# Output projection as seven half-size products for eight, with the norm's row factors moved to the gate products

## The chip, the cores and the metric

The kernel runs on one core of one Trainium2 chip. The metric is the device time of one launch in microseconds; the profiled execution's trace is counted from the start of its span. TensorE multiplies matrices, VectorE (DVE), ScalarE (ACT) and GpSimd (POOL) work on tiles of 128 partitions, and SyncE (SP) and GpSimd issue transfers.

## The reference

One layer of a decoder trunk, with 1024 rows, a width of 1024 and all data in float32. What bears on the change is the end of the mixing sub-layer and the start of the feed-forward:

```python
gates = jax.nn.sigmoid(bg + b_gate[l])
merged = None
for i, y_b in enumerate((y_gla, y_fox, y_mem)):
    term = gates[..., i * D_MODEL:(i + 1) * D_MODEL] * (y_b @ w_branch[l, i])
    merged = term if merged is None else merged + term
x = x + merged @ w_out[l]
h2 = _rmsnorm(x, g_ffn[l])                      # x * rsqrt(mean(x*x) + EPS) * g
x = x + (jax.nn.silu(h2 @ w_ffn_gate[l]) * (h2 @ w_ffn_up[l])) @ w_ffn_down[l]
```

The feed-forward width is 2816. The row factor of the norm (one number for each of the 1024 rows) can be applied to `h2` or, since it is constant along the summed dimension, to the products.

## The kernel before

Activations lie transposed: 128 channels on the partitions, the 1024 rows along the free dimension, in two halves of 512 (`H2`). Every float32 product is three matmuls of 128x512 (`mm3`, lines 844, 846, 848): each operand is split into a rounded high half (a ScalarE cast, line 872) and a low half (a VectorE subtraction, line 873), and high x high, high x low and low x high are summed in one of eight PSUM banks.

The work follows in stages. The merge (`merge_lane`, from about 786 us) multiplies each of the three branches by its projection and by its gate; VectorE forms gate x product (L906), GpSimd adds it to the sum (L907), and for the last branch ScalarE and VectorE split the finished sum (L909, L910). The output projection (`out_half`, 927 to 1019 us) computes for each half of the rows and each of 8 strips of 128 output channels a sum over 8 input strips, adds it to the input tile `x`, stores it (L966) and sums its squares. `half_factors` turns the sums of squares of a half into row factors: narrow matmuls (L978), a power on GpSimd (L103), a diagonal matrix (L980) and one wide matmul (L984). The first half's factors are known during the second half of the projection, and the operands of the first half, B11 and B21, are scaled and split there. The second half's factors are formed after the projection.

The feed-forward works in pairs of 128-channel strips. `products` computes a pair by seven products of half size in place of eight (a Winograd form, its order in `SEQ`): the weights' combinations S1 to S4 are formed and split by `Strip` (its parts `a`, `b`, `c_sums`, `c`, `d` are called between the products of the strip before), and the activations' combinations T1 to T4 are formed once, before the first pair's products use them (`staggered`, `t2_sum` and the functions beside it). Each product sums over 4 input strips, 12 matmuls in all. `Pair.gate` and `Pair.up` read the banks: some products are copied out by ScalarE (L1107), others are added by VectorE; the gate gets Silu (L1126), the up product is multiplied by the gate. `Pair.store` writes seven combinations to memory for the down projection (from 1454 us), which is of the same form.

TensorE's order is written out by hand for the whole kernel; VectorE's from the first product of the feed-forward on, ScalarE's from the third strip on. Before that, VectorE and ScalarE take the order that the planner of the framework sets. Each engine works its queue in order, and a transfer waits in its issuing engine's queue until its tile is free.

## Time and profile before

| what | us |
|---|---|
| median of 3 runs | 1678.42 (1677.35 to 1678.88) |
| the profiled execution | 1678.62 |
| its span | 1676.9 |
| TensorE busy in the span | 1648.2 |
| VectorE busy | 971.4 |
| ScalarE busy | 631.4 |
| GpSimd busy | 185.7 |

The span is the time from the first to the last instruction of the trace; the profiled execution's own time is 1.7 us more. Busy time of TensorE counts overlapping matmuls once, and a matmul's end is modelled, so the distance between starts of matmuls says more than a matmul's duration.

### The profile page before, as it was taken

To read this page: it belongs to the slowest core of one execution; us is meant where nothing else is said; L and a number is where in the kernel's file an instruction comes from. 1 tells how busy PE (TensorE), PEld (TensorE's weight loads), DVE (VectorE), ACT (ScalarE), POOL (GpSimd) and SP (SyncE) were. 2 spreads that over 40 slices of the span, in tenths; PEclk is the share of its full clock that TensorE was granted. 3 is DMA by queue.
4 is the path that set the end of the run, shared out by engine and by line. 5 is a ranking of instruction groups with operands and counts; after the bars stand their busy time and mean duration, and the time that the engine had idled before them with its cause. 6 is when DMAs were issued, how large, how long until landed. Compare 5 with 4: busy or idle time off the path is not lost.

```text
span 1676.9 us, 21943 instructions
## 1 busy us (share of the span) xinstructions
PE 1648.2 (98%) x8411; PEld 1391.6 (83%) x8411; DVE 971.4 (58%) x1537; ACT 631.4 (38%) x1078; POOL 185.7 (11%) x225
## 2 busy tenths in 40 slices
PE   8999999999999999999999999999999999999999
PEld 6889987878879999998887787788888888787877
DVE  8544464154244655554447477866666666748673
ACT  7334454223223444443113344433333333544340
POOL 2000000000010100100044110111121121100000
PEclk9999999999999999999999999999999999999999
DMA  6431121112121221114556631455464455965761
GB/s 226 145 121 63 52 95 59 32 59 87 54 72 53 88 70 54 39 60 156 188 197 199 222 120 57 148 172 163 145 195 150 155 168 168 314 204 195 241 227 57
DMA packets 127321, 220.79 MB, mean 132 GB/s; under 512 B 11552, under 2 KB 71472, under 8 KB 127216
## 3 DMA queue, kind: packets, MB, share of 16 engines
q1 hardware_dynamic: 116256, 183.47, 33.4%
q0 software_dynamic: 10960, 35.92, 6.4%
q8 instruction: 66, 1.08, 0.3%
q14 instruction: 39, 0.32, 0.1%
HBM read 160.30 MB, written 59.05 MB: 131 GB/s over the span
## 4 chain that ended last, share of the span: by engine, by line
PE 85%; DVE 6%; DMA 5%; ACT 2%; issue 1%; SPq 0%; POOL 0%; DVEq 0%; ACTq 0%
PE ps L846 14%; PE ps L848 14%; PE ps L844 14%; PE pm L234 4%; PE pt L155 4%; PE pm L236 4%; PE pm L235 4%; PE pt L156 4%; PE pt L157 4%; PE pm L197 2%; PE pm L201 2%; PE pm L199 2%; PE at L791 1%; DMA hbl<-act_d 1%; DMA raw<-y_d 1%
## 5 line engine op out<-in xcount | busy, mean ns | idle before, releaser
L846 PE MATMUL ps<-hbl,h 128*128 128x512 f32 x520 | 204.1, 393 | 3.4 <-DVE hbl L932 1.8
L844 PE MATMUL ps<-hbh,h 128*128 128x512 f32 x520 | 203.0, 390 | 2.5 <-ACT h L872 1.4
L848 PE MATMUL ps<-hbh,l 128*128 128x512 f32 x520 | 203.7, 392 | 0.5 <-DVE l L873 0.5
L872 ACT CAST h<-w 128x1024 fp32r<-128x1024 f32 (+3 forms) x111 | 97.9, 895 | 175.0 <-DVE w L932 89.8
L234 PE MATMUL pm<-whi,hh 128*128 128x384 f32 (+2 forms) x512 | 162.2, 317 | 0.0
L236 PE MATMUL pm<-whi,hl 128*128 128x384 f32 (+2 forms) x512 | 158.8, 310 | 0.0
L235 PE MATMUL pm<-wlo,hh 128*128 128x384 f32 (+2 forms) x512 | 158.8, 310 | 0.0
L155 PE MATMUL pt<-hh,whi 128*128 128x512 f32 x352 | 142.3, 404 | 0.0
L157 PE MATMUL pt<-hh,wlo 128*128 128x512 f32 x352 | 138.1, 392 | 0.0
L156 PE MATMUL pt<-hl,whi 128*128 128x512 f32 x352 | 138.1, 392 | 0.0
L873 DVE TENSOR_TENSOR l<-w,h 128x1024 fp32r<-128x1024 f32 (+3 forms) x111 | 114.5, 1034 | 37.5 <-ACT h L872 37.4
L846 PEld LDWEIGHTS ps<-hbl,h 128*128 128x128 f32 x520 | 97.8, 188 | 27.1 <-DVE hbl L873 3.5
L844 PEld LDWEIGHTS ps<-hbh,h 128*128 128x128 f32 x520 | 97.8, 188 | 24.1 <-ACT h L872 1.8
L848 PEld LDWEIGHTS ps<-hbh,l 128*128 128x128 f32 x520 | 97.9, 188 | 21.5 <-DVE l L873 1.3
L234 PEld LDWEIGHTS pm<-whi,hh 128*128 128x128 f32 x512 | 96.3, 188 | 2.6
L235 PEld LDWEIGHTS pm<-wlo,hh 128*128 128x128 f32 x512 | 96.4, 188 | 2.5
L846 PE MATMUL ps<-hal,ah 128*128 128x512 f32 x248 | 97.4, 393 | 0.9 <-DVE hal L873 0.7
L848 PE MATMUL ps<-hah,al 128*128 128x512 f32 x248 | 97.2, 392 | 0.0
L844 PE MATMUL ps<-hah,ah 128*128 128x512 f32 x248 | 96.6, 389 | 0.0
L236 PEld LDWEIGHTS pm<-whi,hl 128*128 128x128 f32 x512 | 96.2, 188 | 0.0
L187 DVE TENSOR_TENSOR wlo<-raw,whi 128x512 fp32r<-128x512 f32 (+2 forms) x64 | 48.3, 756 | 78.6 <-ACT whi L186 78.0
L931 DVE TENSOR_TENSOR acc<-ps,acc 128x512 f32<-128x512 f32 x68 | 46.8, 688 | 66.9 <-PE ps L848 66.9
(358 smaller groups left out, 3528.8 us busy)
## 6 DMA issues: line engine op xcount, KB each, us to landing
w<-in_wfd SPq DMA_DIRECT2D x52, 256.0 KB, 3.9
tg<-tg_d SPq DMA_DIRECT2D x24, 512.0 KB, 3.6
w<-in_wfu SPq DMA_DIRECT2D x23, 512.0 KB, 4.7
w<-in_wfg SPq DMA_DIRECT2D x23, 512.0 KB, 4.1
raw<-in_wT SPq DMA_DIRECT2D x22, 512.0 KB, 4.3
tg_d<-gz SPq DMA_DIRECT2D x22, 512.0 KB, 2.9
act_d<-T POOLq DMA_DIRECT2D x44, 256.0 KB, 3.8
sum_d<-w POOLq DMA_DIRECT2D x44, 256.0 KB, 3.4
```

What stands on the lines that cost most here:

```text
L155: nc.tensor.matmul(ps, hi[:, ks], hh[k][:, sl], start=k == 0, stop=False)
L156: nc.tensor.matmul(ps, hi[:, ks], hl[k][:, sl], start=False, stop=False)
L157: nc.tensor.matmul(ps, lo[:, ks], hh[k][:, sl], start=False, stop=k == KT - 1)
L187: nc.vector.tensor_tensor(lo[:, :n], raw[:, :n], hi[:, :n].bitcast(F32), ALU.subtract)
L234: nc.tensor.matmul(ps[:, :n], hh[k][:, ms], hi, start=k == 0, stop=False)
L235: nc.tensor.matmul(ps[:, :n], hh[k][:, ms], lo, start=False, stop=False)
L236: nc.tensor.matmul(ps[:, :n], hl[k][:, ms], hi, start=False, stop=k == KT - 1)
L844: nc.tensor.matmul(ps, hi, a, start=first, stop=False, skip_group_check=more)
L846: nc.tensor.matmul(ps, hi, b, start=False, stop=False, skip_group_check=more)
L848: nc.tensor.matmul(ps, lo, a, start=False, stop=last, skip_group_check=more)
L872: nc.scalar.copy(hi, raw)
L873: nc.vector.tensor_tensor(lo, raw, hi.bitcast(F32), ALU.subtract)
```

## The change

The output projection takes the form of the feed-forward: strips j and j+4 of the output make a pair, and each pair is seven products over 4 input strips in place of eight. The merged sum is split for it into seven combinations: B11, T1, B21 and T2 in the merge's last branch, T3, B22 and T4 during the first strip of the projection (`half_split`). The weights of the projection are laid out by pair and go through `Strip`. The order of VectorE's and ScalarE's work is written out from the projection on. Low halves of weights, square sums and gains are put on a list (`kept`) and issued some products later (`weigh`).

The feed-forward's operands carry only the gain of the norm. Sums of squares for both halves are gathered in one tile `rb`, which becomes the row factors while the first products of the feed-forward run. Each gate product is multiplied by the factor before Silu (VectorE) and after it (GpSimd), the second for the up product's factor. Differences T1, T3 and T4 of the first operands are formed by GpSimd. Tiles `x` are loaded in the order of the pairs, the first strip's (0,1), (4,1) and (4,0) on GpSimd's queue and all others on SyncE's; staging slots for the activations are named by combination (four each) in place of three shared rings. The branch weights are laid out so that the merge takes its strips in the order j, j+4.

The diff, cut to its core (of the functions that it removes, the code is above):

```diff
     ap_ = pool(root, "acc", side="right")
+    fp_ = pool(root, "factors", side="right")
+    rb = fp_.tile([P, S], F32, name="rb")
+    nc.gpsimd.memset(rb, 0.0)
...
+    one = lambda pl, tag, dt=F32R, n=1, w=S: pl.tile([P, w], dt, tag=tag, bufs=n, name=tag)
+    a4 = lambda: (one(xp, "ah"), one(xp, "al"))
+    s2_ = lambda: (one(xp, "s2h"), one(xp, "s2l"))
+    hp1 = pool(root, "h2a")
+    hp2 = pool(root, "h2b")
+    RING = {"B11": hp1, "B21": hp1, "T2": hp2, "T1": hp2}
+    slot = lambda name: tuple(RING[name].tile([P, 512], F32R, tag=name + x, bufs=4, name=name + x) for x in "hl")
+    cell = lambda name: ap_.tile([P, 512], F32, tag="cell", bufs=16, name=name)
+    add = lambda o, a, b: nc.vector.tensor_tensor(o, a, b, ALU.add)
+    sub = lambda o, a, b: nc.vector.tensor_tensor(o, a, b, ALU.subtract)
+    mul = lambda o, a, b: nc.vector.tensor_tensor(o, a, b, ALU.mult)
+    cells = lambda name: {(j, h): cell(name) for js, h in ((range(4), 0), (range(4), 1), (range(4, 8), 1), (range(4, 8), 0))
+                          for j in js}
+    am = cells("am")
+    mg = {}
+    def half_split(name, k, raw, pool_lo=False, late=None):
+        mg[name, k] = hi, lo = slot(name)
+        if pool_lo:
+            nc.scalar.activation(raw, raw, AF.Copy, scale=0.5)
+            nc.scalar.copy(hi, raw)
+            nc.gpsimd.tensor_tensor(lo, raw, hi.bitcast(F32), ALU.subtract)
+            return
+        nc.scalar.activation(hi, raw, AF.Copy, scale=0.5)
+        make = lambda: nc.vector.scalar_tensor_tensor(lo, raw, 0.5, hi.bitcast(F32), ALU.mult, ALU.subtract)
+        make() if late is None else late.append(make)
     def merge_lane():
...
-                    j = jj * 2 + j2
+                    j = jj + 4 * j2
...
-                            nc.gpsimd.tensor_tensor(acc[j][h], acc[j][h], tg[:, s], ALU.add)
-                        if n == 2:
-                            nc.scalar.activation(mgh[j][:, s], acc[j][h], AF.Copy, scale=0.5)
-                            nc.vector.scalar_tensor_tensor(mgl[j][:, s], acc[j][h], 0.5, mgh[j][:, s].bitcast(F32),
-                                                           ALU.mult, ALU.subtract)
+                            nc.gpsimd.tensor_tensor(am[j, h], am[j, h], tg[:, s], ALU.add)
+                    if n == 2 and j2 == 0:
+                        m11, m12 = am[jj, 0], am[jj, 1]
+                        half_split("B11", jj, m11)
+                        sub(m11, m12, m11)
+                        half_split("T1", jj, m11)
+                    if n == 2 and j2 == 1:
+                        m21, m22 = am[jj + 4, 0], am[jj + 4, 1]
+                        half_split("B21", jj, m21)
+                        sub(m11, m22, m11)
+                        half_split("T2", jj, m11)
+                        sub(m12, m22, m12)
+                        nc.gpsimd.tensor_tensor(m21, m21, m11, ALU.subtract)
...
+    wo_a, wo_s = a4(), s2_()
+    ra = wp.tile([P, S], F32, tag="wr", bufs=2, name="raw")
+    rb_, sa = (one(wx, "wx", F32, 2) for i in range(2))
+    nc.sync.dma_start(ra, wout[0][:, 0:S])
+    nc.sync.dma_start(rb_, wout[0][:, S:2 * S])
+    split(*wo_a, ra)
+    add(sa[:, 512:], rb_[:, :512], rb_[:, 512:])
+    sub(sa[:, :512], sa[:, 512:], ra[:, :512])
+    split(*wo_s, sa)
...
+        def split(self, dst, raw, late):
+            if late is None:
+                return split(*dst, raw)
+            nc.scalar.copy(dst[0], raw)
+            late.append([1, lambda: sub(dst[1], raw, dst[0].bitcast(F32))])
+            return dst
+        def a(self, late=None):
             if not self.at:
+                h, l = self.split(a4(), self.ra, late)
                 self.at = {"A11": (h, l, 0), "A12": (h, l, 512)}
+        def b_sums(self, eng=nc.vector):
             sa, ra, rb_ = w4(), self.ra, self.rb
             self.s2, s1 = sa[:, :512], sa[:, 512:]
+            eng.tensor_tensor(s1, rb_[:, :512], rb_[:, 512:], ALU.add)
+            eng.tensor_tensor(self.s2, s1, ra[:, :512], ALU.subtract)
+            return sa
+        def b(self, sa=None, own=True, late=None):
+            sa = self.b_sums() if sa is None else sa
+            h, l = self.split(s2_() if own else a4(), sa, late)
             self.at.update({"S2": (h, l, 0), "S1": (h, l, 512)})
+        def c_sums(self, eng=nc.vector):
             self.sb = w4()
+            eng.tensor_tensor(self.sb[:, 512:], self.ra[:, 512:], self.s2, ALU.subtract)
+            eng.tensor_tensor(self.sb[:, :512], self.ra[:, :512], self.rb[:, :512], ALU.subtract)
+        def c(self, own=True, late=None):
+            h, l = self.split(s3_() if own else s2_(), self.sb, late)
             self.at.update({"S3": (h, l, 0), "S4": (h, l, 512)})
+        def d(self, late=None):
+            h, l = self.split(d2_(), self.rb[:, 512:], late)
             self.at["A22"] = (h, l, 0)
...
+            def then(i, l):
+                def act():
+                    t, r = g[i][l], rb[:, H2[l]]
+                    mul(t, t, r)
+                    nc.scalar.activation(t, t, AF.Silu)
+                    nc.gpsimd.tensor_tensor(t, t, r, ALU.mult)
+                if late is None:
+                    act()
+                else:
+                    late.append(act)
             def last(ps):
+                t, r = cell("t"), rb[:, H2[0]]
+                g[1][0] = t
+                mul(t, ps, r)
+                nc.scalar.activation(t, t, AF.Silu)
+                nc.gpsimd.tensor_tensor(t, t, r, ALU.mult)
+            return products(w, hB, 4, self.reads(g, then, last))
...
+    ve = tc.manual_schedule(engines={mybir.EngineType.DVE, mybir.EngineType.Activation})
+    ve.__enter__()
+    wo = [Strip(w) for w in wout]
+    wo[0].at = {"A11": (*wo_a, 0), "A12": (*wo_a, 512), "S2": (*wo_s, 0), "S1": (*wo_s, 512)}
+    g0, u0, g1 = Strip(wfg[0]), Strip(wfu[0]), Strip(wfg[1])
     pairs = [Pair(), Pair()]
-    g0.b()
-    g0.c_sums()
-    g0.c()
+    late = []
+    x1 = cells("x1")
+    kept = []
+    def load_x(j, h, eng=nc.sync):
+        eng.dma_start(x1[j, h], xT[j][:, H2[h]])
+    def ready(j, h):
+        x, sl = x1[j, h], H2[h]
+        nc.gpsimd.dma_start(x_d[j][h], x)
+        sq = bank8()
+        nc.scalar.activation(sq, x, AF.Square)
+        kept.append([1, lambda: add(rb[:, sl], rb[:, sl], sq)])
+        kept.append([0, lambda: nc.scalar.activation(x, x, AF.Copy, scale=gain(j))])
+    def weigh(age):
+        for y in list(kept):
+            y[0] += 1
+            if y[0] > age:
+                y[1]()
+                kept.remove(y)
+    def out_reads(j):
+        def plus(i, h, last):
+            def read(ps):
+                x = x1[j + 4 * i, h]
+                add(x, x, ps)
+                if last:
+                    ready(j + 4 * i, h)
+            return read
+        return [plus(0, 0, False), plus(0, 0, True), plus(0, 1, False), plus(1, 1, False), plus(1, 1, True),
+                plus(0, 1, True), plus(1, 0, True)]
+    def op(name, k, raw):
+        hops[name, k] = split(*slot(name), raw)
+    def ops_of(name, ks, make=None):
+        where = {"B11": (0, 0), "T1": (0, 0), "T2": (0, 0), "T3": (0, 1), "B21": (4, 0), "T4": (4, 0), "B22": (4, 1)}
+        j, h = where[name]
+        lo = None
+        for k in ks:
+            raw = x1[k + j, h]
+            if make:
+                make(k)
+            hi, l = hops[name, k] = slot(name)
+            nc.scalar.copy(hi, raw)
+            if lo:
+                lo()
+            lo = lambda l=l, raw=raw, hi=hi: sub(l, raw, hi.bitcast(F32))
+        lo()
+    t1 = lambda k: nc.gpsimd.tensor_tensor(x1[k, 0], x1[k, 1], x1[k, 0], ALU.subtract)
+    t2 = lambda k: sub(x1[k, 0], x1[k + 4, 1], x1[k, 0])
+    t3 = lambda k: nc.gpsimd.tensor_tensor(x1[k, 1], x1[k + 4, 1], x1[k, 1], ALU.subtract)
+    t4 = lambda k: nc.gpsimd.tensor_tensor(x1[k + 4, 0], x1[k + 4, 0], x1[k, 0], ALU.subtract)
+    first = range(3)
+    wo[0].load()
+    load_x(0, 0)
+    wo[1].load()
+    mB = lambda name, k: mg[name, k]
+    e1 = None
+    for n in range(4):
+        q = products(wo[n].get, mB, 4, out_reads(n))
+        nxt = wo[n + 1] if n < 3 else g0
+        for i, (_, _, name) in enumerate(SEQ):
+            go(q, 4)
+            weigh(2)
+            if n == 0 and i == 0:
+                los = []
+                for k in range(4):
+                    half_split("T3", k, am[k, 1], late=los)
+                wo[0].b_sums()
+                wo[0].c_sums()
+                wo[0].c(late=kept)
+                for lo in los:
+                    lo()
+                load_x(0, 1, nc.gpsimd)
+                for k in range(4):
+                    half_split("B22", k, am[k + 4, 1], True)
+                weigh(1)
+            if n == 0 and i == 1:
+                wo[0].d(kept)
+            if n == 0 and i == 2:
+                load_x(4, 1, nc.gpsimd)
+            if n == 0 and i == 3:
+                for k in range(4):
+                    half_split("T4", k, am[k + 4, 0])
+                load_x(4, 0, nc.gpsimd)
+            if n == 3:
+                if i == 1:
+                    ops_of("B11", first)
+                    for k in first:
+                        t1(k)
+                if i == 3:
+                    ops_of("B21", first)
+                    e1 = w4(F32R), w4(F32R)
+                    gb = g0.b_sums(nc.gpsimd)
+                    g0.c_sums(nc.gpsimd)
+                if i == 4:
+                    ops_of("B11", [3])
+                    split(*e1, e_raw)
+                    u0.at = {"A11": (*e1, 0), "A12": (*e1, 512)}
+                    for k in first:
+                        t3(k)
+                if i == 5:
+                    ops_of("T1", first)
+                if i == 6:
+                    g0.b(gb, late=kept)
+            if i == 2:
+                nxt.a(kept)
+            if i == 4 and n < 3:
+                nxt.b(late=kept)
+            if i == 5 and n < 3:
+                nxt.c_sums()
+                nxt.c(late=kept)
+            if i == 6 and n < 3:
+                nxt.d(kept)
+            if i == 6 and n == 2:
+                e_raw = w4()
+                nc.sync.dma_start(e_raw, wfu[0][:, 0:S])
+            for m in [1] if n == 0 and i == 3 else [2] if n == 0 and i == 6 else [3] if n == 1 and i == 2 else []:
+                for j, h in ((m, 0), (m, 1), (m + 4, 1), (m + 4, 0)):
+                    load_x(j, h)
+            if i == 6 and n < 3:
+                (wo[n + 2] if n < 2 else g0).load()
+        go(q)
...
+    q0, q1, q2 = pairs[0].gate(g0.get), pairs[0].up(u0.get), None
+    rcol = cp.tile([P, KT], F32, name="rcol")
+    weigh(2)
+    t1(3)
+    t3(3)
     g0.d()
...
+    u0.load()
+    ops_of("T2", range(3), t2)
+    hops["B21", 3] = h, l = slot("B21")
+    split_evac(x1[7, 0], gain(7), h, l)
+    ops_of("T1", [3])
+    ops_of("T2", [3], t2)
     go(q0, 4)
+    weigh(0)
+    for k in range(4):
+        t4(k)
+    go(q1, 4)
+    ps = bank8()
+    for t in range(KT):
+        nc.tensor.matmul(ps[:, t:t + 1], rb[:, t * P:(t + 1) * P], ones[:, 0:1], start=True, stop=True)
+    rsqrt_(rcol, ps[:, :KT], KT, 1.0 / D)
+    nc.vector.tensor_tensor(rb.rearrange("p (t c) -> p t c", c=P), ident.unsqueeze(1).broadcast_to([P, KT, P]),
+                            rcol.unsqueeze(2).broadcast_to([P, KT, P]), ALU.mult)
     go(q0, 4)
     go(q1, 4)
+    pst = [bank8(), bank8()]
+    for ps, sl in zip(pst, H2):
+        nc.tensor.matmul(ps, ones, rb[:, sl], start=True, stop=True)
+    for ps, sl in zip(pst, H2):
+        nc.scalar.copy(rb[:, sl], ps)
+    u0.b(own=False)
+    go(q0, 4)
+    ops_of("T3", range(4))
+    g0.c()
+    late.pop(0)()
+    go(q0, 4)
     u0.c_sums()
+    for act in late:
+        act()
+    late = None
+    go(q1, 4)
+    u0.d()
+    go(q1, 4)
+    ops_of("B22", range(4))
+    u0.c(own=False)
+    g1.load()
     go(q0, 4)
+    ops_of("T4", range(4))
     go(q1, 4)
+    g1.a()
     go(q0, 4)
+    b = g1.b_sums()
     go(q1, 4)
+    g1.b(b)
+    g1.d()
     go(q0, 4)
+    g1.c_sums()
     go(q1, 4)
     g1.c()
     ve.__exit__(None, None, None)
```

## Rows read from the trace of the kernel before

**Rows 1.** Page, engines over the span: busy us (share of the span) xinstructions.
```profile
PE 1648.2 (98%) x8411; PEld 1391.6 (83%) x8411; DVE 971.4 (58%) x1537; ACT 631.4 (38%) x1078; POOL 185.7 (11%) x225
```

**Rows 2.** Table by stretch: window, length, engines' busy us (xinstructions), clock, DMA share, GB/s.
```profile
886.00:927.00 41.00, 39.66 (x174) 32.49 (x174) 29.23 (x32) 12.82 (x18) 19.86 (x15) 1.00 0.58 193
927.00:1019.00 92.00, 90.23 (x394) 72.94 (x394) 58.49 (x76) 38.71 (x51) 12.34 (x18) 1.00 0.47 167
1019.00:1090.00 71.00, 65.84 (x274) 50.92 (x274) 61.07 (x93) 32.11 (x49) 8.42 (x13) 0.98 0.32 98
1090.00:1455.00 365.00, 365.00 (x1604) 300.64 (x1603) 245.21 (x334) 126.47 (x184) 65.84 (x106) 1.00 0.55 175
1455.00:1677.00 222.00, 211.02 (x911) 169.51 (x909) 140.70 (x202) 80.85 (x127) 2.17 (x4) 1.00 0.59 194
```

**Rows 3.** Timeline of TensorE, 945 to 1049: start, duration, engine, line, operation, count.
```profile
945.01 0.39 PE L846 MATMUL ps<-mgl,h 128*128 128x512 f32 x1
...
950.45 0.39 PE L846 MATMUL ps<-mgl,h 128*128 128x512 f32 x1
...
1022.43 1.05 PE L978 MATMUL ps<-ones,ssq 128*128 128x1 f32 x8
...
1026.17 1.02 PE L984 MATMUL ps<-dg,ones 128*128 128x512 f32 x2
...
1048.33 0.63 PE L844 MATMUL ps<-hbh,h 128*128 128x512 f32 x1
1048.75 0.63 PE L846 MATMUL ps<-hbl,h 128*128 128x512 f32 x1
```

**Rows 4.** Waits of TensorE, 927 to 1022, then 1019 to 1090: us, times, longest.
```profile
PE ps L844 <- ACT ah L872: 1.2, 1, 1.2
...
PE ps L846 <- DVE hbl L932: 1.8, 2, 1.0
PE ps L844 <- ACT h L872: 1.4, 1, 1.4
```

**Rows 5.** Chain of waits, 920 to 945: start, duration, what.
```profile
927.00 6.04 DMA w<-in_wout
```

**Rows 6.** DMA issues, 915 to 945: count, KB each, median us to landing.
```profile
x<-in_xT SPq DMA_DIRECT2D x6, 256.0 KB, 3.6
```

**Rows 7.** Timeline of VectorE, 891 to 1039.
```profile
891.94 1.94 DVE L910 SCALAR_TENSOR_TENSOR mgl<-acc,mgh 128x512 fp32r<-128x512 f32 x2 [1.48 <-ACT mgh L909]
...
1004.96 0.68 DVE L931 TENSOR_TENSOR x<-x,ps 128x512 f32<-128x512 f32 x1
1005.55 1.21 DVE L873 TENSOR_TENSOR l<-w,h 128x1024 fp32r<-128x1024 f32 x1
...
1038.97 1.23 DVE L873 TENSOR_TENSOR al<-w,ah 128x1024 fp32r<-128x1024 f32 x1 [1.12 <-ACT ah L872]
```

**Rows 8.** Timeline of GpSimd, 889 to 1025.
```profile
889.95 2.54 POOL L907 TENSOR_TENSOR acc<-acc,tg 128x512 f32<-128x512 f32 x2 [3.84 <-DVE tg L906]
895.42 3.52 POOL L907 TENSOR_TENSOR acc<-acc,tg 128x512 f32<-128x512 f32 x2 [2.94 <-issue]
...
997.65 0.54 POOL L966 DMA_DIRECT2D x_d<-x  x1 [10.27 <-DVE x L931]
...
1023.77 1.04 POOL L103 TENSOR_TENSOR rcol<-rcol,mhalf 128x4 f32<-128x4 f32 x1 [2.54 <-DVE rcol L102]
```

**Rows 9.** Groups of ScalarE over the span: busy us, mean ns, idle before.
```profile
L872 ACT CAST h<-w 128x1024 fp32r<-128x1024 f32 x69 | 72.2, 1047 | 166.8 <-DVE w L932 89.8 <-PE ps L846 68.8 <-issue 7.8
L1126 ACT ACTIVATE t<-t 128x512 f32<-128x512 f32 x33 | 20.9, 632 | 91.0 <-DVE t L931 91.0
```

**Rows 10.** Table by stretch, one pair of feed-forward strips.
```profile
1120.00:1158.00 38.00, 38.00 (x168) 31.33 (x167) 25.00 (x34) 12.71 (x18) 6.51 (x12) 1.00 0.51 159
```

**Rows 11.** Waits of all engines, 1090 to 1450: us, times, longest.
```profile
DVE al L873 <- ACT ah L872: 47.4, 19, 2.9
...
DVE l L873 <- ACT h L872: 28.4, 28, 1.2
```

More of the change, by code (lines that the diff above doesn't have):

```diff
@@ L1133, in last, with then @@
                 mul(u[1][0], ps, g[1][0])
-            return products(w, hB, 4, self.reads(u, lambda i, l: mul(u[i][l], u[i][l], g[i][l]), last))
+            def then(i, l):
+                act = lambda: mul(u[i][l], u[i][l], g[i][l])
+                if late is None:
+                    act()
+                else:
+                    late.append(act)
+            return products(w, hB, 4, self.reads(u, then, last))
         def store(self, p):
             (b11, b12), (b21, b22) = self.u
-            t1, t2, t3, t4 = (cell("T") for i in range(4))
+            t1, t2, t3, t4 = self.T or [cell("T") for i in range(4)]
             sub(t1, b12, b11)
@@ L1191, in left @@
     def left(name, n):
[L1192 to L1227 removed]
+        free[name] += n
         feed()
@@ L1258, in staggered @@
-    def staggered(name, work, between=None):
-        last = None
-        for k in range(4):
-            raw = work(k)
-            lo = raw_lo(name, k, raw)
-            if last:
-                last()
-            last = lo
-            if between and k == 1:
-                between()
-        last()
-    def t2_sum(k):
-        t3, t2 = x1[k + 4][1], t2s[k]
-        mul(t3, t3, rb)
-        add(t2, t3, x1[k][0])
-        return t2
-    def t1_sum(k):
-        b12, t1 = x1[k][1], x1[k][0]
-        mul(b12, b12, rb)
-        sub(t1, b12, t1)
-        return t1
@@ L1283, in b22_sum @@
-    def b22_sum(k):
-        add(x1[k][1], x1[k + 4][1], x1[k][1])
-        return x1[k][1]
-    def t4_sum(k):
-        sub(x1[k + 4][0], x1[k + 4][0], t2s[k])
-        return x1[k + 4][0]
-    ve = tc.manual_schedule(engines={mybir.EngineType.DVE})
-    ve.__enter__()
-    go(q0, 4)
-    next(fac)
-    go(q0, 4)
-    rb = next(fac)
-    t2s = [t[:, s] for t in (w4(), w4()) for s in H2]
-    ring = lambda name: RING.get(name, (hp2, "hb", 16))
-    RING = {"B11": (hp1, "ha", 8), "B21": (hp1, "ha", 8)}
@@ L1408, in trunk @@
         go(q)
+    pairs[NP - 1].T = [cell("T") for i in range(4)]
     for s_, (b, jj, p0, n) in enumerate(steps):
```

222 lines of the change are left out of this document (30 added, 192 removed).

## The prediction, on record before the change was run

> **What bounds the kernel now.** I read the page's busy line first: TensorE is busy 98% of the span [rows 1], so only two things can move the time: fewer matmuls, or fewer holes between them. The table by stage comes next [rows 2]. It shows where holes are: from 1090 to 1455 us TensorE is busy all of 365.00 us, while the stretch of the output projection (927 to 1019) and the first products of the FFN (1019 to 1090) have some. I measure holes against the pitch of matmuls that wait for nothing: from the start at 945.01 to the one at 950.45 there are 24, so 0.2267 each [rows 3]; the body's 365.00 us over 1604 records, 0.2276, agrees [rows 2]. The projection has 394 records in 92.0 us. Ten are row-factor matmuls: the 8 narrow ones take 1.05 and the two wide ones 1.02 [rows 3], 2.1 together. The other 384 take 384 x 0.2267 = 87.0, so 92.0 - 87.0 - 2.1 = 2.9 us are lost there. In 1019 to 1090 there are 274 records: 264 x 0.2267 = 59.9, plus 2.1, leaves 71.0 - 62.0 = 9.0 us lost.
>
> The waits of TensorE name the causes [rows 4]: in the projection the second strip's weights, whose load can start only when the merge's buffers come free (a landing of 6.04 us in the chain of waits [rows 5]); in the FFN's start the halves of T2 that VectorE forms (L932, after the row factors are known) and weights. After the waits of the start the matmuls stand 0.42 to 0.43 apart for a while [rows 3]: that is 1.2 GHz instead of 2.4 GHz, the mean granted clock of the stretch is 0.98 [rows 2], and eight such matmuls cost 8 x 0.2 = 1.6 us of the 9.0.
>
> **The change, part by part.**
>
> *Matmuls removed.* Before: 16 output halves x 8 x 3 = 384. After: 4 pairs x 7 products x 4 x 3 = 336. 48 x 0.2267 = 10.9 us less. Nothing hides TensorE, so this counts in full. The factor matmuls stay as many (8 narrow, 2 wide) and move behind the projection: 0.
>
> *Merge (last branch).* VectorE is busy 29.23 of the last 41.00 us [rows 2]. It gains three subtractions per pair (12 in all; the half splits are 16 as before) and for the first strip two sums and one more low half: 12 x 0.69 + 2 x 0.6 + 1.2 = 10.7, so 39.9 of 41. Durations: an operation of 128x512 takes 0.68 to 0.69 and an independent one follows its neighbour after 0.60; a low half of 128x1024 takes 1.23 [rows 7]. Beside GpSimd it is dearer: two neighbouring half subtractions took 1.94 instead of 1.3 while GpSimd added [rows 7, 8]. TensorE does not wait for it inside the merge, since its eight banks hold four strips; but VectorE arrives at the projection 0 to 3 us late. I take 1.5.
>
> *First strip of the projection* (t = 0: end of the merge's matmuls; a product is 12 x 0.2267 = 2.7 us, so B21 is wanted at 2.7, T2 at 5.4, T3 at 10.9, B22 at 13.6, T4 at 16.3). The tail of the merge is two gated products 1.3, GpSimd's two adds 2.54 for the pair [rows 8], then B21's last piece, the T2 difference, its halves, m12: VectorE is through at about 6.5, with its lateness 8. Last pieces of B21 and T2 are wanted 2.0 after their products start, 4.7 and 7.5: about 0.5 lost. The raw weights and the first x tile are issued at t = 0 and land at about 6 [rows 5], an x tile alone after 3.6 [rows 6], and VectorE's next operation adds product 0 to that x: 8.6. Then four sums for S2, S3, S4 (2.5): 11.1; the high half of S3/S4 on ScalarE (1.05 [rows 9]) 12.2; four low halves of T3 (2.4) 13.5; low half of S3/S4 (1.2) 14.7. Its first use is 0.45 after 10.9 plus the 0.5: 11.8. Lost: 2.9. I take 2.5, since the sums may start while x lands. Then T4: its low halves stand on VectorE behind the add into x tile (4,1). That tile's load is issued by GpSimd, behind the four low halves of B22 that GpSimd forms (1.27 each, from two ScalarE operations of 0.63 [rows 9] each, starting after the S3 cast: 12.2 + 5.0 + 1.3 = 18.5) and an x store (0.54 [rows 8]). Issue 19.6, landing 2 to 3.6 later, 22.4; add 23.1, first T4 half 23.7. T4 is wanted at 16.3 + 3.0 lost so far + 0.5 = 19.8. Lost: 3.9; if the loads of weights land as early as 3.6, 1. I take 3.0. With 0.2 for each restart the strip loses 6.6; from both sides 2 to 10. Before, the projection lost 2.9: the part costs +3.7.
>
> *Strips 1 to 3.* VectorE: 7 adds, 4 square adds, 4 sums (15 x 0.65) and 3 wide plus 1 narrow low half (4.2) = 14 of 19.1 us; loads come a strip ahead. 0. In strip 3 ten more low halves (6.9) and GpSimd's differences (10 x 1.27) stand beside it: VectorE ends it 0 to 3 us late; I take 1.5.
>
> *FFN start* (t = 0: end of the projection). The factor no longer stands before T2: operands carry the gain only, the factor's square adds go to VectorE, and the factor is wanted only by the gate products' evacuations. What is late next is B21's last piece, x tile (7,0), the last product. In VectorE's queue stand before it: its add 0.7, two square adds 1.3, a low half 0.6 behind ScalarE's queue (about 2 of waiting), three T2 differences and their low halves 3.9, then itself 0.7: 9.3, with the lateness 10.8. TensorE has B11 for gate and up (24 x 0.2267 = 5.4), 1.05 of narrow matmuls and 9 of B21 (2.0): wanted at 8.5. Lost: 2.3. Then 0.7 + 2.7 of B21 until the wide factor matmul, at 14.2. Its operand is behind T1's and T2's last pieces 2.6, S2's low half 1.2, 0.2, GpSimd's power (1.04 for 4 columns [rows 8]; taken 1.5 for 8) and 1.2 for the diagonal: 10.8 + 6.7 = 17.5. Lost: 3.3. Restarts 0.4 and one spell of 1.2 GHz as in [rows 3], 1.6: 7.6. From both sides: 2 (VectorE not late, ScalarE never waited for) to 13 (each GpSimd operation delays VectorE by a full 1.27, two spells). Before 9.0: the part gives -1.4.
>
> *Gate products.* Per pair of FFN strips four more VectorE products (0.69) and four on GpSimd (1.27). VectorE is busy 25.00 of 38.00 us per pair [rows 10], so 27.8; GpSimd 6.51, so 11.6. Gate results are used a whole strip (19 us) later. 0; the cover is VectorE's 10 us of slack per pair, and without it the second rival below. Weight halves are formed up to a product earlier: 0. *Down projection*: the staging slots go by name; as many tiles are loaded early (7 of 28), some of them names that are wanted late. Loss before: 222.0 - 911 x 0.2267 = 15.5 with the tail [rows 2]; after -2 to +3, I take 0.
>
> **A rule weighed.** In [rows 7, 8] VectorE's half subtraction and GpSimd's add, both reading SBUF, lengthened each other: 1.94 for two instead of 1.3, 3.52 instead of 2.54 elsewhere. The Trainium skill ("SBUF — State Buffer", section "Who interferes with whom") says that a VectorE instruction with two SBUF inputs and a GpSimd instruction that reads SBUF exclude each other for a whole instruction. The trace's delay, 0.6 on VectorE, agrees in kind and is less than a whole 1.27. By the rows the four new GpSimd products cost VectorE 4 x 0.6 = 2.4 a pair; by a whole instruction each, 5.1.
>
> **Sum.** -10.9 + 3.7 - 1.4 = -8.6, against the profiled execution's 1678.62 (span 1676.9 and 1.7 around it), 0.2 above the median: **1670.0 us**.
>
> **Rivals.**
> 1. *The stalls go altogether* (0.20): the first strip loses 2 and the start 2: -10.9 - 0.9 - 7.0 = -18.8, 1659.8. For it: the factor is off the path and both engines' orders are written out. Against: every low half still passes VectorE, busy 61.07 of 71.00 in the start [rows 2].
> 2. *VectorE becomes the bound of the FFN's body* (0.08), slower. Place: every pair from 1090 on. Its 25.0 busy, the 75.8 us that it waits for ScalarE's casts there [rows 11] (7.9 per pair), 2.8 of new products and 5.1 of exclusion are 40.8, over the 38.0 that TensorE needs. From 38.0 on each pair is late; 2.8 x 10 pairs = 28: 1670 + 28 = 1698. Against: the low halves are issued a product after the casts now, which takes most of the 7.9 away (32.9 left), and the rows show 2.4, not 5.1. The skill's rule above is what gives the 5.1.
> 3. *The new stalls eat the gain* (0.14): strip 0 loses 10 and the start 13: -10.9 + 7.1 + 4.0 = +0.2, 1678.8. Place: VectorE's queue behind x tile (4,1) and behind B21's last piece. For it: GpSimd issues that load after its own arithmetic. Against: it takes the worst end of both.
> 4. *Matmuls dearer than counted* (0.02): 0.0068 more for each of 336 would be 2.3; no more than part of the range.
>
> **How the numbers follow.** The forecast's own case, 1664 to 1675, has 0.56. 0.2% (3.4 us) is about what a measurement of this kernel tells from no change. Faster by more: 0.56 + 0.20 + 0.01 = 0.77; within: 0.14; slower: 0.09. The range 1661 to 1678 leaves out half of rival 1, rival 2 and half of rival 3.
>
> **What would show it.** 336 matmuls instead of 384 on the projection's operands; TensorE's waits in strip 0 at S3/T3 and T4, released by VectorE; one at B21 and one at the wide factor matmul in the FFN's start; no TensorE wait in the body. It would be wrong if TensorE waits in the body, or if strip 0 or the start loses over 10 us or under 3.

## The result, and the profile after

The changed kernel takes 1692.0 us (median of 4 runs, 1689.9 to 1694.1) against 1677.9 for the kernel before: a ratio of 1.0084, 95% interval 1.0066 to 1.0101. It is slower by 14 us where the prediction had it faster by 8.6. The profiled execution took 1691.49, its span 1689.7.

The page's engines, as in [rows 1]: 48 instructions fewer on TensorE, as foretold, 58 more on VectorE, 71 more on GpSimd.

```profile
PE 1641.5 (97%) x8363; PEld 1386.9 (82%) x8363; DVE 1039.6 (62%) x1595; ACT 642.0 (38%) x1104; POOL 296.1 (18%) x296
```

The table by stretch, columns as in [rows 2]: window, length, busy us of PE, PEld, DVE, ACT, POOL (instructions), granted clock, DMA share, GB/s.

```profile
886.00:926.40 40.40, 39.75 (x174) 32.59 (x175) 33.66 (x38) 11.18 (x17) 22.95 (x16) 1.00 0.34 115
926.40:949.00 22.60, 14.54 (x52) 10.18 (x51) 19.75 (x25) 10.15 (x17) 12.59 (x10) 0.92 0.54 184
949.00:1004.00 55.00, 52.71 (x225) 43.07 (x224) 42.11 (x59) 27.65 (x41) 9.66 (x15) 0.97 0.50 163
1004.00:1030.00 26.00, 21.68 (x88) 17.21 (x86) 23.41 (x24) 11.52 (x20) 16.51 (x14) 0.93 0.15 53
1030.00:1069.00 39.00, 27.54 (x112) 20.50 (x112) 29.69 (x37) 20.01 (x33) 13.55 (x9) 0.91 0.20 68
...
1100.00:1464.00 364.00, 364.00 (x1603) 300.63 (x1602) 282.29 (x366) 124.66 (x179) 126.61 (x145) 1.00 0.54 173
```

Read it by its holes. The FFN's body (last row) has none, and the merge (first row) has 0.65 us, no more than the 1.34 of [rows 2]. All of the loss lies between, in three places: the first strip of the projection, its last strip (from 1004) and the FFN's start (from 1030). The waits of TensorE from 926 to 1100 (us in all, times, longest) name who was late, to be held against [rows 4]:

```profile
PE ps L844 <- DVE x L891: 9.9, 3, 4.3
PE ps L844 <- ACT B21h L242: 6.2, 1, 6.2
PE ps L1347 <- DVE rb L1341: 2.9, 1, 2.9
PE ps L844 <- ACT B11h L908: 2.8, 1, 2.8
```

The largest, `DVE x L891`, is no operand of the waiting matmul. L891 is the add by which VectorE reads a finished product out of its PSUM bank; the next product but one writes the same bank and must wait for that read. The prediction did not have this wait.

Sizes, by the prediction's own measure (time less 0.2267 per matmul, and 2.1 for each ten records of factor matmuls; all twenty now stand in the FFN's start). The projection's first and FFN's first matmul in the timeline of TensorE (start, duration, engine, line, operation, count):

```profile
926.54 0.39 PE L844 MATMUL ps<-B11h,ah 128*128 128x512 f32 x1
...
1024.48 0.39 PE L844 MATMUL ps<-B11h,ah 128*128 128x512 f32 x1
```

336 matmuls took 97.9 us and need 76.2: 21.8 lost, 15.5 of it up to 965 (first strip) and 6.3 in the last strip. From there to 1100, 16.2 are lost. Before it was 2.9 and 9.0. So -10.9 + (21.8 - 2.9) + (16.2 - 9.0) = +15.2; 0.8 less is lost in the body and 0.8 less in the down projection, which leaves 13.6. The two profiled executions differ by 12.9; the projection's start, at 926.54 after 927.27, is the other 0.7.

### The profile page after: what moved, and what is told of

Read it like the earlier page. It is cut to its first block, busy times and chain, and to the rows that moved or that the text cites. A ratio compares the mean times of both kernels' runs of the same rounds, so it can differ in the third digit from the quotient of the medians.

```text
span 1689.7 us, 22126 instructions
## 1 busy us (share of the span) xinstructions
PE 1641.5 (97%) x8363; PEld 1386.9 (82%) x8363; DVE 1039.6 (62%) x1595; ACT 642.0 (38%) x1104; POOL 296.1 (18%) x296
## 4 chain that ended last, share of the span: by engine, by line
PE 79%; DVE 8%; DMA 6%; issue 3%; ACT 2%; POOL 2%; SPq 0%; DVEq 0%; ACTq 0%; POOLq 0%
PE ps L846 12%; PE ps L848 12%; PE ps L844 12%; PE pm L234 4%; PE pt L155 4%; PE pm L236 4%; PE pm L235 4%; PE pt L156 4%; PE pt L157 4%; PE pm L197 2%; PE pm L201 2%; PE pm L199 2%; DMA T1l<-act_d 1%; PE at L791 1%; DMA w<-sum_d 1%
## 5 line engine op out<-in xcount | busy, mean ns | idle before, releaser
L891 DVE TENSOR_TENSOR acc<-ps,acc 128x512 f32<-128x512 f32 x68 | 47.0, 691 | 66.5 <-PE ps L848 66.5
L186 ACT CAST whi<-raw 128x512 fp32r<-128x512 f32 (+2 forms) x64 | 42.9, 673 | 93.0 <-PE pm L199 60.8
L157 PEld LDWEIGHTS pt<-hh,wlo 128*128 128x128 f32 x352 | 66.1, 188 | 14.7
L155 PEld LDWEIGHTS pt<-hh,whi 128*128 128x128 f32 x352 | 66.2, 188 | 8.8 <-issue 1.7
L891 DVE TENSOR_TENSOR t<-ps,t 128x512 f32<-128x512 f32 x66 | 45.2, 686 | 45.2 <-PE ps L848 35.2
L156 PEld LDWEIGHTS pt<-hl,whi 128*128 128x128 f32 x352 | 66.3, 188 | 7.1
L932 POOL TENSOR_TENSOR am<-am,tg 128x512 f32<-128x512 f32 x32 | 48.7, 1543 | 113.5 <-DVE tg L931 110.0
L1065 ACT COPY t<-ps 128x512 f32<-128x512 f32 x66 | 38.3, 582 | 78.7 <-PE ps L848 78.7
L844 PE MATMUL ps<-T3h,s3h 128*128 128x512 f32 x144 | 57.6, 400 | 8.4 <-DVE x L891 7.6
L165 DVE TENSOR_TENSOR gz<-pt,rbc 128x512 f32<-128x512 f32 x44 | 30.2, 689 | 56.6 <-PE pt L157 54.0
L844 PE MATMUL ps<-B21h,ah 128*128 128x512 f32 x144 | 57.0, 396 | 6.2 <-ACT B21h L242 6.2
```

Of the source, the lines that this page charges most:

```text
L155: nc.tensor.matmul(ps, hi[:, ks], hh[k][:, sl], start=k == 0, stop=False)
L156: nc.tensor.matmul(ps, hi[:, ks], hl[k][:, sl], start=False, stop=False)
L157: nc.tensor.matmul(ps, lo[:, ks], hh[k][:, sl], start=False, stop=k == KT - 1)
L844: nc.tensor.matmul(ps, hi, a, start=first, stop=False, skip_group_check=more)
L891: add = lambda o, a, b: nc.vector.tensor_tensor(o, a, b, ALU.add)
L932: nc.gpsimd.tensor_tensor(am[j, h], am[j, h], tg[:, s], ALU.add)
```

## The experiments

Each is an edit of the changed kernel; times are medians, ratios stand against runs of the kernel before beside it. Where values are left out it is said.

### GpSimd's share: differences on VectorE, and left out

Every low half and difference has two inputs in SBUF. In the last strip GpSimd forms the first gate strip's sums and T1's differences beside VectorE's low halves. VectorE's timeline of the changed kernel (start, duration, ...; in brackets idle before), then GpSimd's:

```profile
1007.41 6.47 DVE L892 TENSOR_TENSOR B11l<-x,B11h 128x512 fp32r<-128x512 f32 x3 [1.22 <-ACT B11h L1235]
1013.80 0.67 DVE L891 TENSOR_TENSOR x<-x,ps 128x512 f32<-128x512 f32 x1
```
```profile
1007.30 1.30 POOL L1016 TENSOR_TENSOR w<-w,w 128x512 f32<-128x512 f32 x1
1008.55 1.74 POOL L1015 TENSOR_TENSOR w<-w,w 128x512 f32<-128x512 f32 x1
...
1010.83 2.49 POOL L1241 TENSOR_TENSOR x<-x,x 128x512 f32<-128x512 f32 x2
```

Three low halves take 6.47 us. Behind them stands the add at 1013.80 that reads T2's bank, and on TensorE T3's first product waits for that add:

```profile
1009.91 0.39 PE L848 MATMUL ps<-T1h,s2l 128*128 128x512 f32 x1
1014.62 0.66 PE L844 MATMUL ps<-T3h,s3h 128*128 128x512 f32 x1 [4.33 <-DVE x L891]
1015.09 0.63 PE L846 MATMUL ps<-T3l,s3h 128*128 128x512 f32 x1
1015.51 0.63 PE L848 MATMUL ps<-T3h,s3l 128*128 128x512 f32 x1
```

(The 0.42 between the last two starts, for 0.23, is the 1.2 GHz level after the engine stood still: the granted clock from 1014.6 to 1017 is 0.53. The strip loses 1.8 beyond the wait.) Two runs ask whether GpSimd is the cause. First, the same operations on VectorE:

```diff
-t1 = lambda k: nc.gpsimd.tensor_tensor(...)      # t3, t4 likewise
+t1 = lambda k: nc.vector.tensor_tensor(...)
-gb = g0.b_sums(nc.gpsimd); g0.c_sums(nc.gpsimd)
+gb = g0.b_sums(); g0.c_sums()
```

> The ten operations that GpSimd does in the last strip of the projection (T1 and T3 of three pieces, the four sums of the first gate weights) and those of the FFN's start (T1, T3 of the last piece, T4) go to VectorE. Theory X (exclusion): there GpSimd holds up VectorE's two-input operations for whole instructions (three low halves of B11 took 6.47 us where 1.9 is usual, three of B21 4.81), the adds that read the banks come late behind them, and the next product into the same bank waits (4.3 us at T3 of the last strip). Without GpSimd these go: VectorE gains 14 x 0.6 = 8.4 us of work but loses about 13 of blocking, the wait at T3 falls from 4.3 to 0-2 and the time falls by 3 to 7, to about 1687. Theory L (load): VectorE has too much work there in any case; 8.4 us more of it lengthen the waits, 1695 to 1700.

Measured: 1690.9, ratio 1.0082 (1.0067 to 1.0097). The same three low halves now take 1.90:

```profile
1008.64 1.90 DVE L892 TENSOR_TENSOR B11l<-x,B11h 128x512 fp32r<-128x512 f32 x3 [1.22 <-ACT B11h L1235]
```

The last strip's wait falls from 4.33 to 1.56 and B21's from 6.2 to 0.3, but the factor matmuls wait 2.2 and 6.1 in their place. So GpSimd does lengthen VectorE's work, and still the time stays: VectorE now does it all itself and is as late at the next operand. Second, leaving T1's, T3's and T4's differences out (the operands are wrong then; the four sums stay on VectorE, as in the first run):

```diff
-t1 = lambda k: nc.gpsimd.tensor_tensor(...)      # t3, t4 likewise
+t1 = lambda k: None
```

> As the run with the differences on VectorE, but the differences T1, T3 and T4 are left out (their operands are split undifferenced; the output is not the reference's) and only the four weight sums go to VectorE. Theory X: no exclusion and only 2.6 us more for VectorE: no wait at T3 of the last strip (6.3 us with the slow clock behind it), the wait for B21's last piece at the FFN's start falls from 6.2 to 2-4: 1677 to 1683. Theory L: the low halves, square adds and reads are still there, the waits stay within 2 us: 1690 or more. Theory S (the gain in place waits for the store of x, 2.8-3.3 us each time): the waits stay too, since the store and the gain stay.

Measured: 1683.4, 1.0041 (1.0026 to 1.0056): 8.6 us come back. It is the differences that count, on whichever of the two engines; the run takes away their work and the waits on them together and doesn't part the two.

### The bank rule alone

```diff
-first = bk not in banks
+first = fresh or bk not in banks      # fresh in the projection: a new bank for each product
```

Each product starts its own bank, so what was summed in a bank is left out of the result.

> In the projection each of the seven products of a strip gets a bank of its own in place of adding into one of three (so sums of products are left out and the output is not the reference's; the same number of matmuls and of reads). Theory B (bank): three waits of TensorE, 3.3 and 2.3 us in the first strip and 4.3 in the last, end with a VectorE add that reads the bank into which the next product goes; with own banks they go, and what is late next is an operand: S3's low half in the first strip (about 2 us), T4's halves (1-2). With the slow clock that follows two of them (1.9 and 1.8) 8 to 11 us less: 1680 to 1684. Theory O (operands): the operands are as late as the banks, and the time stays within 2 us of 1692.

Measured: 1690.6, 1.0081 (1.0066 to 1.0096). The bank waits go; TensorE then waits 1.5 for T3's weights, 1.3 for T4's cast, 3.6 for the FFN's first weights and 6.2 for B21 as before. The projection loses 7.8 less, and the FFN's start 6 more. So the rule says where VectorE's lateness is felt first; without it the lateness is felt one stage later.

### The merge's tail

VectorE's timeline at the end of the changed kernel's merge:

```profile
923.01 0.68 DVE L931 SCALAR_TENSOR_TENSOR tg<-tg,ps 128x512 f32<-128x512 f32 x1
...
925.48 1.29 DVE L892 TENSOR_TENSOR am<-am 128x512 f32<-128x512 f32 x2 [1.19 <-POOL am L932]
926.87 1.60 DVE L909 SCALAR_TENSOR_TENSOR T2l<-am,T2h 128x512 fp32r<-128x512 f32 x1
928.39 1.27 DVE L931 SCALAR_TENSOR_TENSOR tg<-tg,ps 128x512 f32<-128x512 f32 x2
931.60 1.08 DVE L909 SCALAR_TENSOR_TENSOR B11l<-am,B11h 128x512 fp32r<-128x512 f32 x1 [1.93 <-ACT B11h L908]
...
933.39 1.28 DVE L931 SCALAR_TENSOR_TENSOR tg<-tg,ps 128x512 f32<-128x512 f32 x2
```

The last gate product is at 933.39, 6.9 after TensorE had left the merge. Each strip goes from VectorE to GpSimd, to ScalarE and back, and the next gate product stands in the queue behind that round trip, while VectorE idles (1.19, 1.93). In the kernel before the last gate product waited for TensorE, which left the merge at 927.27:

```profile
927.25 1.28 DVE L906 SCALAR_TENSOR_TENSOR tg<-tg,ps 128x512 f32<-128x512 f32 x2 [0.69 <-PE ps L848]
```

Some of the changed kernel's rows are also long: T2's and B11's low halves take 1.60 and 1.08 for 0.68, beside these operations of GpSimd:

```profile
926.31 1.61 POOL L944 TENSOR_TENSOR am<-am 128x512 f32<-128x512 f32 x1 [0.87 <-DVE am L892]
...
929.63 2.50 POOL L932 TENSOR_TENSOR am<-am,tg 128x512 f32<-128x512 f32 x2
```

Leaving differences out of the merge:

```diff
-sub(m11, m12, m11)                    # and sub(m11, m22, m11), sub(m12, m22, m12), GpSimd's m21 - m11
```

The 16 differences are left out, so T1 to T4 have wrong values; the halves are formed as before.

> The sixteen differences in the merge's last branch (12 on VectorE, 4 on GpSimd) are left out: the half splits take the undifferenced sums (the output is not the reference's). Theory M (VectorE late in the merge): VectorE is behind by 6 us at the merge's end because of these differences and of the waits in its queue that they bring, so B11's last piece is 2.8 us late and the clock falls; without them the waits at B11, B21 and T2 (5.7 + 0.6 + 1.1 with the slow clock) go, and T3 comes earlier: 1682 to 1686. Theory P: GpSimd's queue is the cause, where a load of an x tile waits for T2's low half between the merge's adds; that load stays, and the time stays within 2 us.

Measured: 1685.6, 1.0056 (1.0039 to 1.0073): 6.4 us come back. The last gate product is now 2.6 after TensorE's leaving the merge (925.20), not 6.9:

```profile
927.78 1.27 DVE L931 SCALAR_TENSOR_TENSOR tg<-tg,ps 128x512 f32<-128x512 f32 x2
```

Four of the differences were GpSimd's, so the run doesn't part VectorE's own work from what GpSimd's operations add to it. Writing VectorE's order by hand, each gate product ahead of the halves of the strip before (the edit also loads the last branch's weights a strip ahead and splits the projection's first weights inside it):

```diff
+if n == 2 and jj == 1: vm.__enter__()          # VectorE in the order written, from here
...
-half_split("B11", jj, m11); sub(m11, m12, m11); half_split("T1", jj, m11)
+while pend: pend.pop(0)()
+pend.append(upper)                             # the same, one strip later; lower likewise
```

> All work as in the changed kernel, but VectorE's order in the merge's last branch is written out: the gate products of a strip stand before the halves and differences of the strip before it. Theory Q (order): in the changed kernel a strip's gate product stands in VectorE's queue behind the previous strip's chain, gate product 1.3, two adds on GpSimd 2.5, a cast 0.6, a low half 0.7 and a difference 0.7, 5.8 us or more in all where TensorE needs 5.45 for a strip, so VectorE falls behind by some us; out of the loop, the waits at B11, B21 and T2 of the first strip (7.4 with the slow clock) go to 0-2, T3 comes 1-2 earlier: 1683 to 1686. Theory W (work): VectorE has too many instructions there in any order; the run with the differences left out was faster because work was left out, and this one stays within 2 us of the changed kernel's 1692.

Measured: 1746.0, 1.0409 (1.0393 to 1.0424). Low halves of the merge's weights now come late before the order by hand begins (34 us of waits of TensorE from 792 on), so the time decides nothing. The last branch tells more: in the run of that order with others (below) the first gate products of three pairs of strips start at 942.57, 956.19 and 969.74 (between them two of the differences):

```profile
942.57 1.29 DVE L957 SCALAR_TENSOR_TENSOR tg<-tg,ps 128x512 f32<-128x512 f32 x2 [4.16 <-issue]
...
945.27 1.60 DVE L892 TENSOR_TENSOR am<-am 128x512 f32<-128x512 f32 x1
...
951.89 1.78 DVE L892 TENSOR_TENSOR am<-am 128x512 f32<-128x512 f32 x1
...
956.19 1.27 DVE L957 SCALAR_TENSOR_TENSOR tg<-tg,ps 128x512 f32<-128x512 f32 x2
...
969.74 1.27 DVE L957 SCALAR_TENSOR_TENSOR tg<-tg,ps 128x512 f32<-128x512 f32 x2
```

That is 13.6 us a pair, where TensorE needs 48 x 0.2267 = 10.9. In this order too VectorE can't keep up: it is busy 12.1 of the 13.6 from 942.57 on. But five of its operations in each pair take 1.3 to 1.8 for 0.69 beside GpSimd's operations, 4.1 us in all; without that it would be busy some 8 us (an estimate, 12.1 less 4.1). Whether its own work or GpSimd's beside it makes it late in the merge is not shown; no run takes GpSimd's operations away alone.

### A transfer as the cause

```diff
-load_x(0, 1, nc.gpsimd)               # and (4, 1), (4, 0)
+load_x(0, 1)                          # issued by SyncE
```

> The three loads of x tiles that GpSimd issues go to SyncE's queue; nothing else. Theory P: GpSimd waits at these loads for VectorE's halves (1.1 us before the last two pairs of adds) and so passes VectorE's lateness on; without them the wait for B11's last piece falls from 2.8 to about 1 and the time by 2 to 4. Theory Q: the loads wait for what VectorE is late with anyway; within 1.5 us of 1692.

Measured: 1692.4, 1.0093 (1.0077 to 1.011). No gain: where GpSimd's queue lets these loads start is not what the first strip waits for.

### Both at once

Both sets of differences left out, values as said above:

> Leaves out part of the computation: the 16 differences that the merge's last branch forms and the 12 differences T1, T3, T4 of the FFN's input; the sums of the first gate strip stay, on VectorE. It puts together two edits whose prices alone were -8.6 us (FFN differences) and -6.4 us (merge's differences). Theory A (all of the loss is VectorE's lateness, made by these extra operations at two places that do not touch each other): the prices add up, 1692.0 - 15.0 = 1677.0, within 1.5 us, about the time of the kernel before; 24 extra microseconds of TensorE's waits shrink to about 10. Rival B (one lateness handed on along the queue): taking the merge's away already helps the later places, so both together give clearly less than the sum, 1680 to 1682.

Measured: 1676.0, 0.9984 (0.9975 to 0.9992), 16 us below the changed kernel: 8.6 + 6.4 = 15.0 add up, as far as the intervals tell (by the ratios the two gave back 7.2 and 4.7, both together 16.8). TensorE's largest waits, 920 to 1100:

```profile
PE ps L844 <- DVE x L891: 5.8, 3, 3.5
PE ps L844 <- ACT B21h L242: 2.4, 1, 2.4
PE ps L1343 <- DVE rb L1337: 2.0, 1, 2.0
```

Here 10.4 are lost in the projection (9.5 in the first strip, 0.9 in the last) and 11.1 in the start. The two edits act at different places: without the merge's differences alone the first strip loses 10.1, the last 5.9 and the start 17.8; without the others alone it is 17.3, 0.9 and 11.1.

### Can an order give it back?

At the FFN's start B21's last piece stands behind the T2 work. Moving it ahead, and the wide factor matmuls behind T2's first product (T3's and T4's differences and A22's halves go behind the factors):

```diff
-t1(3); t3(3); g0.d(); u0.load(); ops_of("T2", range(3), t2)
 hops["B21", 3] = h, l = slot("B21"); split_evac(x1[7, 0], gain(7), h, l)
+t1(3); u0.load(); ops_of("T2", range(3), t2)
...
+go(q0, 4)
 pst = [bank8(), bank8()]
```

> Only the FFN's start is in another order: B21's last piece is split first on ScalarE and VectorE, in front of T2's differences; T3's and T4's last differences and A22's halves come behind the row factors; TensorE takes the last quarter of the two B21 products behind the other three, and the wide factor matmuls after the first T2 product. Theory Q (order): the wait for B21's last piece (6.2, with restart and slow clock 9.3) goes, the one for the wide factor matmul (2.9) too; next late is T2 by 2 to 5: 1683 to 1687. Theory W (work): VectorE has this much to do before T2 and the wait moves there in full: 1690 to 1693.

Measured: 1691.5, 1.0087 (1.0069 to 1.0105). B21's wait and the wide factor's are gone, and T2's product waits as long:

```profile
1036.48 0.39 PE L848 MATMUL ps<-B21h,w 128*128 128x512 f32 x1
1042.85 0.79 PE L844 MATMUL ps<-T2h,s2h 128*128 128x512 f32 x1 [5.98 <-ACT t L1065]
```

L1065 is ScalarE's copy out of B11's bank, queued behind T2's casts, which wait for VectorE. With the copies ahead of the third and fourth cast:

```diff
-ops_of("T2", range(3), t2); ...; go(q0, 4); go(q1, 4)
+ops_of("T2", range(2), t2); go(q0, 4); ops_of("T2", [2], t2); go(q1, 4); ...
```

> Computes all. Only the order at the FFN's start changes, as in the earlier run with B21's last piece first and the factor's wide product after T2's first, but ScalarE's copies of the first products' bank now stand after the second and third T2 cast, not after the fourth. Theory Q (the 5.98 us at the T2 product in that run were the in-order queue: the copy of the bank stood on ScalarE behind casts that wait for VectorE): the T2 wait falls to 0 to 2 us, B21 and the wide factor matmul stay without waits, and the time is 1686 to 1688.5. Rival W (VectorE simply has too much to do between the projection and T2, whatever the order): the wait comes back at T2's operands or at the products after it, 1690 to 1692.

Measured: 1691.1, 1.007 (1.0056 to 1.0084). The bank wait shrinks to 0.3; T2's operands, S2's low half and the factor wait instead. (T1's last piece takes T2's values in this run and in the second below: it was formed after T2 had overwritten its source. Operations and queues are as many.) All orders together, first with the merge by hand, then without:

> All work of the changed kernel, in another order and on other engines: the merge's order by hand, x loads on SyncE, the FFN's start as in that run, T4's casts of the first strip one product earlier, the last strip's T1 differences and the four sums of the first gate weights on VectorE, and T3's differences (GpSimd) behind the row factors. Theory Q: each wait of the changed kernel between 926 and 1068 is one of queue order or of exclusion, and 18 to 24 of the 36 us lost go: 1668 to 1675, below the kernel before (1677). Theory W: VectorE's work between the merge and the second pair is too much for any order, and the time stays over 1682.

Measured: 1743.3, 1.0388 (1.0373 to 1.0404), of no use because of the same late weights in the merge (34 us).

> Computes all. Theory A's repair without touching the merge: the order of the FFN's start as in the other run; T1's differences and the first gate strip's sums on VectorE instead of GpSimd; T3's differences moved from the last strip to the FFN's start; T4's casts of the first strip one product earlier than the gains that wait for the x store. Expected from the single runs: the last strip's 4.5 us go to 1 to 2.5, T4 of the first strip 2.45 to 2, the start's 15 to 4 to 8; the merge's tail and T3 of the first strip stay. 1677 to 1682. Rival W: the work put on VectorE makes it later and the start's waits stay at over 10 us: 1686 to 1690.

Measured: 1686.8, 1.0048 (1.0036 to 1.0061). With T1's last piece in its right place:

> Computes all: the run of all orders (v3), with T1's last piece formed before T2's last overwrites its source, which is the order it should have had; nothing else differs. Theory A and rival W say the same of it, 1685 to 1688, since the operations and their queues are as many; more than 1689 would mean that this one order decides, under 1684 that T1's place was holding T2 up.

Measured: 1684.7, 1.0045 (1.0031 to 1.0059), the best that computes all. In its profile the first strip, the last strip and the FFN's start lose 1.7 less each, 5.1 in all; the projection also begins 2.1 earlier, which the edit doesn't explain. Two runs went further: T3's low halves behind the add that reads the bank, the wide factor matmuls behind T1's first product, and in the second GpSimd's order written out as well:

> The same as the other kernel of this call but with GpSimd's order left to the planner; it computes all. Theory A: GpSimd forms the T3 differences as early as they are ready, beside VectorE's T2 work, and its power behind them; 1 to 3 us more than the other. Rival W: no difference over 1 us.

> Computes all. As the run of all orders, with three more: GpSimd's order is written out too from the projection on, so that the factor's power stands ahead of the T4 and T3 differences; T1's last piece is formed before T2's last; the wide factor product stands behind T1's first product, and in the first strip the low halves of T3 are issued after the add that reads the bank T3 needs. Theory A (the start's and the first strip's waits are places in in-order queues): the wide factor wait of 2.1 and the slow clock behind it go, T3's 3.25 in the first strip falls under 1.5, and the time is 1680 to 1684. Rival W (VectorE has as much to do as TensorE there, so the waits only move): 1685 to 1688.

Measured: 1689.0, 1.0064 (1.005 to 1.0077), and 1692.4, 1.0085 (1.0071 to 1.0099). In both, T3's first product waits some 2 us for the bank and then about 4 for the low halves that were put back, where it waited 3.3 in all; in the second TensorE also waits 3.6 for weights of the FFN. The order of the same work gave back 5 to 7 of 14 us, by removing GpSimd's overlap and two queue places together, which no run parts; no version that computes all reaches the kernel before.

## Why the prediction was wrong

- *Matmuls removed, -10.9*: right, 336 for 384 at the same pitch.
- *Gate products, body and down projection, 0*: right. The body loses nothing (364.00 of 364.00). VectorE is busy 282.29 of 364, 29.5 per 38 us; 25.00 + 2.8 was foretold and 30.2 with the rows' exclusion. Rival 2 is out.
- *Merge, "VectorE arrives at the projection 0 to 3 us late; I take 1.5"*: this step failed first. The sum of its work was near: 33.66 busy up to 926.4 and 10.8 of the merge's work behind it are 44.5, where the 39.9 foretold and the 3.1 that stood behind the merge before make 43.0. But I read a queue that is 97% full as one that is 1.5 late. It also has to wait for GpSimd and ScalarE once per strip (it idles 6.7 of the last 40.4 us), and there is no room left to make that up: the last gate product comes 6.9 after the merge, and VectorE is through with the merge 15.3 after it, where 8 was foretold. Leaving the differences out gives 6.4 back.
- *First strip, 6.6*: 15.5. Of the 8.9 too little, the merge's lateness is 6.0 (9.5 are lost without any differences). The waits in that run were near the forecast, 1.1 at B21, 1.8 at T3 and 3.5 at T4 for 0.5, 2.5 and 3.0, though T3 and T4 wait for banks, where I had only listed operands. The rest is what follows the waits, restarts and the 1.2 GHz level, 3.1 for 0.6; I had counted that level in the start alone.
- *Strips 1 to 3, "0"*: right for 1 and 2; strip 3 lost 6.3, 4.33 of it in one wait. I had summed VectorE's work over a strip and found slack; what counted was that one product's time passes between the end of a bank's product and the next use of that bank.
- *A rule weighed.* I let [rows 7, 8] decide, 0.6 us for each overlapped operation. By the Trainium skill ("SBUF — State Buffer", section "Who interferes with whom") the one engine blocks the other for a whole instruction. In the last strip the trace agrees with that: 6.47 - 1.90 = 4.57 more on VectorE beside GpSimd operations of 5.4 us within it, 1.1 for each of the four. In the body it was 0.4 for each (29.5 - 27.8 = 1.7 for four), under the rows' figure. The row of the 1.94 was of operations that met in part. The trace of the kernel before also has one that met whole, beside the 3.52 of [rows 8], 1.77 for 0.69:

```profile
897.72 1.77 DVE L910 SCALAR_TENSOR_TENSOR mgl<-acc,mgh 128x512 fp32r<-128x512 f32 x1
```

- *FFN start, 7.6*: 16.2. B21's wait was 6.2 for 2.3, the wide factor's 2.9 for 3.3. B21's last piece was there 16.0 after the projection, not 10.8; it was wanted at 9.6, not 8.5, since the narrow matmuls of both halves (sixteen records) took 1.95 and not 1.05:

```profile
1030.16 1.95 PE L1339 MATMUL ps<-ones,rb 128*128 128x1 f32 x16
...
1040.47 0.79 PE L844 MATMUL ps<-B21h,ah 128*128 128x512 f32 x1 [6.17 <-ACT B21h L242]
```

  In the run without the differences the two waits are 2.4 and 2.0, near what was foretold, and the stretch loses 11.1: its 3.5 above the forecast are mostly S2's waits at the up product (1.0 and 0.5), two waits of the second gate strip (0.7 and 0.6) and 0.5 at the narrow matmuls, which I did not have.
- Rival 3 had the sign and the place but not the price: it took the worst of both strips' bounds, 10 and 13, and both were exceeded, since each was bounded with VectorE nearly on time. Losses of over 10 in strip 0 and in the start were also the prediction's own sign of being wrong.

So one thing runs through every place: VectorE is behind at the merge's tail, catches up in strips 1 and 2, and falls behind again from the last strip on. The two sets of differences hold 16 us, more than the whole 14 lost. Without them the kernel would be 0.16% faster, not 0.5%: the projection would lose 10.4 for 6.6 and the start 11.1 for 7.6, by the slow clock and the waits that I had not listed. What was not tried: the bank rule lifted in a kernel that computes all, and the merge without GpSimd's operations beside VectorE's.

## What to carry to other kernels

Where a product accumulates on in a bank that another engine must read in between, list that read among the wait's candidates, at its place in the reading engine's queue: its cover is one product, not one strip. An engine at 97% of a stretch with a round trip in each step is not "1.5 late": here it idled 6.7 us in those round trips and ended 6.9 late, and the next stage inherits the lateness until there is slack (strips 1 and 2, which lost nothing). Work moved to GpSimd was no relief for VectorE here, where both read SBUF in the same stretch (1692.0 us with it on GpSimd, 1690.9 on VectorE): price it as if VectorE did it.

## What the runs showed of the hardware

Beside four GpSimd operations three VectorE subtractions of 128x512 took 6.47 us for 1.90: 1.1 us more for each of the four, close to the 1.27 that one takes. And the spells at 1.2 GHz follow waits: after a wait of 4.33 us the next matmuls start 0.42 apart for 0.23 (after one of 2.3 us, at 958.22, they did not), and the stretches with waits have granted clocks of 0.91 to 0.97 where those before and after have 1.00.
